# First stage of a hybrid decoder segment on a transposed copy of x, norm factors applied behind the products, and TensorE's order in the attention written by hand

## The chip, the cores and the metric

One core of a Trainium2 chip runs the whole program, a two-layer decoder segment over 1024 tokens of width 1024. The metric is the device time of one execution in microseconds, the median of three runs. TensorE (PE) multiplies, VectorE (DVE), ScalarE (ACT) and GpSimd (POOL) work element by element, and SyncE (SP) issues nearly all DMAs.

## The reference

Layer 0 is sliding-window attention (16 query heads, 2 key heads of 64, window 128, a learned sink per head, partial rotary), layer 1 a gated linear recurrence. Both sit between two RMS norms:

```python
for layer in range(DEPTH):
    h = rmsnorm(x, pre_norm_w[layer])
    y = attention_mixer(h, ...) if layer % 2 == 0 else hgrn2_mixer(h, ...)
    x = x + rmsnorm(y, post_norm_w[layer])

def rmsnorm(x, w):   # float32
    return x * rsqrt(mean(x * x, -1, keepdims=True) + 1e-6) * w

def attention_mixer(h, positions, w_in, b_in, sinks, w_out, b_out):
    q, k, v, z = split(h @ w_in + b_in)          # 1024, 128, 128, 1024 columns
    q, k = partial_rope(q), partial_rope(k)      # first 16 of 64 dims
    o = sliding_window_gqa(q, k, v, sinks)       # 128-query blocks, softmax with sink
    return (o * silu(z)) @ w_out + b_out
```

The factor `rsqrt(mean(x*x))` of a norm is one number per token. A projection is linear in it, so it can be multiplied in before the product or behind it, ahead of the bias.

## The kernel before, in words

All products are float32 made of three float32r matmuls: each operand is held as a high part and a low part (`act[k, half]` as `acth`/`actl`, weights as `whi`/`wlo`), and `product` (line 189) issues high x high, low x high and high x low for one block `k` of 128 rows of the 1024 that are summed over. The tokens are cut into two halves of 512. A unit is one PSUM tile of 128 features x 512 tokens: `proj_feat` runs eight products, 24 matmuls, into it. Weights come in slots of 128 x 512, by DMA into one of four `wraw` buffers; POOL (slots under 20) or ACT makes the high part, DVE subtracts for the low part, into one of ten buffers. A slot is split as soon as a buffer comes free (`advance`, `used`).

The order of instructions on an engine is set by a scheduler in the recording layer, by a simulated timeline and priorities (`hp()` and `tc.high_priority` move instructions ahead). `InOrder` pins an engine's instructions to the order in which they are written; before, this is used on DVE alone, in the head (line 87 is its line in the profile).

The head, before: 128 tokens at a time, the rows of x are loaded (`x_load`), ACT squares and sums them (line 978 for the first half, 225 for the second), POOL takes the power -1/2 (line 217), DVE multiplies the rows (`norm_rows`), TensorE transposes them (line 237: four 128 x 128 transposes for one block `k` of a half, 32 for a half), and ACT and DVE split the transposed block into `acth` (line 179) and `actl` (line 87 or 180), times the norm weight. The units of the head are the values `v_unit(0)`, the four query units `q_unit(0, ct, 0)` of the first key head and the keys `k_unit(0)`. A branch on a flag (`values_load`), computed from the recurrence's bounds in `cst`, stands ahead of both layers: each engine reads it before it goes on.

The attention, before: for each key head `g` and block `b` of 128 queries, two steps (`par`), 32 in all. A step is: scores (eight matmuls, lines 530 and 531), copy and mask on ACT and DVE, maximum, four exponentials on ACT (line 545), division on DVE (line 548), four transposes (line 551), split into `pT` on ACT and DVE, four or five masks on POOL (up to line 570), and the heads (four matmuls, lines 573 to 577), whose result ACT and DVE (lines 578, 579) add up. Between the steps the list `fill` supplies 30 units: keys, values and queries of the second half, all queries of the second key head, and 16 gate units `z_unit`; the numbers in `at` say how many are written behind each block. Four gate units are left behind the attention. `g_split` then makes `act` out of the gated heads, and `out0_first` starts the output projection.

## Time and profile before

| | |
|---|---|
| median of 3 runs | 907.21 us (907.04 to 907.98) |
| profiled execution | 907.38 us, its span 905.7 us |
| granted TensorE clock | 0.997 |
| busy: PE, DVE, ACT, POOL | 883.6, 556.7, 378.2, 330.6 us |
| instructions of PE | 5342 matmuls and transposes |
| moved by DMA | 78.63 MB |

The span runs from the first instruction to the last. A row of the windows gives the busy time of each engine in a stretch and the number of instructions; a row of the timeline begins with the start and the time taken in microseconds, and ends with the idle time before it and what ended it. A busy TensorE need not be at its peak, since matmuls overlap.

### The profile page before, as it was taken

The numbers are of one execution on the slowest core, as the hardware profiler recorded it, in microseconds if no ns is written. First come the engines' busy times: TensorE is split into PE (matmuls) and PEld (weight loads), VectorE is DVE, ScalarE is ACT, GpSimd is POOL, SyncE is SP. The second block draws the span as 40 slices with busy tenths as digits, with TensorE's granted clock in tenths as the row PEclk, the third lists the DMA queues.
The fourth block names the chain that finished last, engine by engine and source line by source line (L and its number), as shares of the span: only waits on it lengthen the run. The fifth ranks groups of instructions, "written<-read, shape, count | busy, mean of one in ns | idle before, by whom it ended". The sixth has DMA issues, their size and how long they took to land.

```text
span 905.7 us, 14367 instructions
## 1 busy us (share of the span) xinstructions
PE 883.6 (98%) x5342; PEld 738.6 (82%) x5342; DVE 556.7 (61%) x919; ACT 378.2 (42%) x982; POOL 330.6 (37%) x498
## 2 busy tenths in 40 slices
PE   5999999999999999999999999999999999999996
PEld 4888888888878888878888888888888788888885
DVE  6879888777788336762278774336877824252333
ACT  6526667666666232543322332423334224251211
POOL 5504466667776003420053522115425433220011
PEclk9999999999999999999999999999999999999998
DMA  8546364522212234531211010210111003031053
GB/s 284 159 146 184 105 184 128 154 56 76 85 37 81 81 93 138 172 122 42 87 50 34 25 47 1 69 58 28 35 47 47 1 1 93 1 110 78 24 185 121
DMA packets 53608, 78.63 MB, mean 87 GB/s; under 512 B 4824, under 2 KB 25048, under 8 KB 53528
## 3 DMA queue, kind: packets, MB, share of 16 engines
q1 hardware_dynamic: 53248, 77.48, 27.6%
q8 instruction: 44, 0.72, 0.3%
q14 instruction: 36, 0.29, 0.1%
q10 hardware_dynamic: 280, 0.13, 0.1%
HBM read 58.89 MB, written 16.88 MB: 84 GB/s over the span
## 4 chain that ended last, share of the span: by engine, by line
PE 76%; DVE 8%; POOL 6%; issue 5%; ACT 2%; DMA 2%; SPq 0%; POOLq 0%; ACTq 0%; DVEq 0%
PE psmm L189 63%; POOL rstd L217 2%; PE psk L853 1%; PE pso L866 1%; PE pss L530 1%; PE pss L531 1%; PE pso L868 1%; PE pst L551 1%; POOL ms L215 1%; ACT sm L545 1%; DVE actl L180 1%; PE pst L847 1%; PE pst L880 1%; DMA o<-in_x 1%; PE psd L804 1%
## 5 line engine op out<-in xcount | busy, mean ns | idle before, releaser
L189 PE MATMUL psmm<-acth,whi 128*128 128x512 f32 x528 | 208.8, 396 | 0.6 <-DVE ql L378 0.3
L189 PE MATMUL psmm<-acth,wlo 128*128 128x512 f32 x528 | 207.8, 394 | 0.2 <-POOL wlo L155 0.2
L189 PE MATMUL psmm<-actl,whi 128*128 128x512 f32 x528 | 207.7, 393 | 0.0
L189 PE MATMUL psmm<-whi,acth 128*128 128x512 f32 (+1 forms) x520 | 202.7, 391 | 0.5 <-DVE y L632 0.5
L189 PE MATMUL psmm<-wlo,acth 128*128 128x512 f32 (+1 forms) x520 | 200.7, 387 | 0.0
L189 PE MATMUL psmm<-whi,actl 128*128 128x512 f32 (+1 forms) x520 | 200.6, 388 | 0.0
L155 DVE TENSOR_TENSOR wlo<-wraw,whi 128x512 fp32r<-128x512 f32 x126 | 94.8, 765 | 93.4 <-ACT whi L154 86.6
L189 PEld LDWEIGHTS psmm<-acth,whi 128*128 128x128 f32 x528 | 99.3, 188 | 20.9 <-DVE qf L706 0.8
L189 PEld LDWEIGHTS psmm<-acth,wlo 128*128 128x128 f32 x528 | 99.2, 188 | 19.9 <-POOL wlo L155 0.6
L189 PEld LDWEIGHTS psmm<-whi,acth 128*128 128x128 f32 x520 | 97.7, 188 | 20.4 <-DVE y L632 0.8
L189 PEld LDWEIGHTS psmm<-actl,whi 128*128 128x128 f32 x528 | 99.2, 188 | 18.2
L189 PEld LDWEIGHTS psmm<-whi,actl 128*128 128x128 f32 x520 | 97.7, 188 | 19.6
L189 PEld LDWEIGHTS psmm<-wlo,acth 128*128 128x128 f32 x520 | 97.8, 188 | 19.2
L154 ACT ACTIVATE whi<-wraw 128x512 fp32r<-128x512 f32 x112 | 70.2, 631 | 87.3 <-PE psmm L189 67.4
L545 ACT ACTIVATE sm<-sm,st 128x129 f32<-128x129 f32 x128 | 50.0, 393 | 56.0 <-DVE st L543 56.0
L714 POOL TENSOR_SCALAR gate<-gate,lbt 128x512 f32<-128x512 f32 x16 | 17.7, 1108 | 119.1 <-ACT gate L712 108.5
L927 DVE TENSOR_TENSOR y<-psmm,wpost 128x512 f32<-128x512 f32 (+1 forms) x17 | 11.2, 660 | 53.7 <-ACT jk L926 50.5
L217 POOL TENSOR_TENSOR rstd<-ms,nhalf 128x1 f32<-128x1 f32 (+1 forms) x48 | 41.7, 870 | 3.8
L562 POOL TENSOR_SCALAR_AFFINE_SELECT mY<-pT 64x256 fp32r<-64x256 f32 x56 | 28.6, 511 | 36.7 <-ACT pT L554 31.0
L926 ACT ACTIVATE jk<-psmm 128x512 f32<-128x512 f32 (+1 forms) x17 | 9.7, 571 | 67.0 <-PE psmm L189 67.0
L179 ACT ACTIVATE acth<-pst,cst 128x512 fp32r<-128x512 f32 x48 | 29.6, 693 | 12.7 <-PE pst L237 12.7
L565 POOL TENSOR_SCALAR_AFFINE_SELECT mY<-pT 64x256 fp32r<-64x256 f32 x64 | 31.8, 496 | 6.9 <-ACT pT L554 1.6
(219 smaller groups left out, 1420.2 us busy)
## 6 DMA issues: line engine op xcount, KB each, us to landing
wraw<-in_w SPq DMA_DIRECT2D x132, 256.0 KB
QS<-qd SPq DMA_DIRECT2D x16, 512.0 KB
xr<-in_x SPq DMA_DIRECT2D x8, 512.0 KB
x1d<-xn SPq DMA_DIRECT2D x8, 512.0 KB
xr<-x1d SPq DMA_DIRECT2D x8, 512.0 KB
out_dram<-xn SPq DMA_DIRECT2D x16, 256.0 KB
xh<-in_x SPq DMA_DIRECT2D x4, 512.0 KB
qd<-qh SPq DMA_DIRECT2D x8, 256.0 KB
```

Source lines behind the costliest of these rows:

```text
L154: nc.scalar.activation(hi, raw, AF.Copy)
L155: W["split_ins"][i] = (nc.gpsimd if on_pool else v).tensor_tensor(lo, raw, hi.bitcast(F32), op=ALU.subtract)
L179: ins = nc.scalar.activation(hi, ps, AF.Copy, scale=scale)
L180: W["actl"][k] = v.scalar_tensor_tensor(lo, ps, scale, hi.bitcast(F32), op0=ALU.mult, op1=ALU.subtract)
L189: W["mm"] = nc.tensor.matmul(ps, a, b, start=(k == 0 and i == 0), stop=(k == NK - 1 and i == 2))
L217: W["rstd"] = keep(nc.gpsimd.tensor_tensor(r, m, nhalf[:, :width], op=ALU.pow))
L545: nc.scalar.activation(sm[:, h, :], sm[:, h, :], AF.Exp, bias=nm[:, h:h + 1], scale=0.125, accum_out=dn[:, h:h + 1])
L562: nc.gpsimd.affine_select(mY[r, :, :64], src[64:, :, :64].bitcast(F32), [[0, 4], [-1, 64]], ALU.is_gt, 0.0, base=0, channel_multiplier=1)
L565: nc.gpsimd.affine_select(mY[r, :, 64:], src[:64, :, 64:].bitcast(F32), [[0, 4], [1, 64]], ALU.is_ge, 0.0, base=0, channel_multiplier=-1)
L714: nc.gpsimd.tensor_scalar(dst, dst, ol, lb, op0=ALU.mult, op1=ALU.add)
L926: nc.scalar.activation(jk[:, c0:c1], ps, AF.Square, scale=D ** -0.5, accum_out=ss)
L927: v.tensor_tensor(y[:, c0:c1], ps, wpost[:, c * 512 + c0:c * 512 + c1], op=ALU.mult)
```

## The change

Head. The host also hands in x transposed (`xt`), and the head loads blocks of it straight into the layout that the products need. `act[k, 0]` is made of unnormalised x times the norm weight. Both first units (values and the first query unit) run side by side, block by block, as `xt` and the first four weight slots land; of slots 0 and 2 the first 128 columns are split first. The rows of x are still loaded, for the sums of squares alone; the factors of 512 tokens are spread over 128 partitions by four transposes of a broadcast column (`spread`), into `rb0` and `rb1`. A unit of the first half is multiplied by `rb0` when it leaves PSUM (`scaled`, one more DVE instruction for each of 18 units). For the second half `xt1` itself is multiplied by `rb1` (`scaled_half`, eight DVE instructions). The rows' buffers are `xt1` and the rotary tables' space, so these are filled only behind the sums. In the head all five engines keep the written order.

Attention. `attn` is cut in three: `scores`, `turned` (transposes, split, masks) and `heads_out`. `later` puts a part on a list with the number of products behind which it is issued: step `i` has its scores behind 25 + 7.3 i products, its transposes 11 and its heads 21 products further on. TensorE's order is pinned as written, through the first four output units. The four gate units that stood behind the attention are now inside it; a gate unit with `p >= 4` now writes the gate alone, and the heads of the second key head are multiplied in behind it, for all eight blocks (before: four). `g_split` of the first half is inside too, and weight splits have no raised priority while the list runs. `tw` has two buffers (one before), `sm` two (three before), `ql` one (two before).

```diff
+        def split_first(i, c0, c1, act=False):
+            hi, lo, raw = whi[i][:, c0:c1], wlo[i][:, c0:c1], wraw[i][:, c0:c1]
...
-                with hp():
-                    on_pool = i in (2, 3)
+                with ExitStack() if W["plan"] else hp():
...
+            W["pos"] += 1
+            while W["plan"] and W["plan"][0][0] <= W["pos"]:
+                W["plan"].pop(0)[1]()
+
+        def later(d, f, block=99):
+            W["plan"].append((W["pos"] + d, f, block))
+            W["plan"].sort(key=lambda e: e[0])
...
+            def scaled(ps, half, t=None):
+                if half:
+                    return ps
+                if t is None:
+                    t = qp.tile([P, 512], F32, tag="th", bufs=2, name="sc")
+                v.tensor_tensor(t, ps, rb0, op=ALU.mult)
+                return t
...
+                def spread(rs, rb):
+                    pt = pp.tile([P, 512], F32, tag="o", name="psr")
+                    for j, r in enumerate(rs):
+                        pe.transpose(pt[:, j * P:(j + 1) * P], r.to_broadcast([P, P]), ident)
+                    ac.activation(rb, pt, AF.Copy)
+
+                def scaled_half(xt, rb, half):
+                    v.on = True
+                    for k in range(NK + 2):
+                        if k < NK:
+                            x = xt[:, k, :]
+                            v.tensor_tensor(x, x, rb, op=ALU.mult)
+                            ac.activation(act[k, half][0], x, AF.Copy, scale=cst[:, C_PRE + k:C_PRE + k + 1])
+                        if k > 1:
+                            act_low(k - 2, half, xt[:, k - 2, :], cst[:, C_PRE + k - 2:C_PRE + k - 1])
+                    v.on = False
...
-                    last = transpose_half(hn0, 0, C_PRE, {2: lambda: advance(4)})
...
+                    for k in range(NK):
...
+                            act_from_psum(k, 0, o0v[:, k, :], cst[:, C_PRE + k:C_PRE + k + 1])
...
+                        for u in range(2):
+                            c = (k % 4) * P
+                            product(first[u], k, weight(2 * u, k // 4, c, c + P), act[k, 0])
+                            used(2 * u + k // 4)
...
+                    rs0 = [row_rstd(sp, rows[0][j], jkb) for j in range(4)]
...
+                    ps2 = proj_feat(q_first(0, 2), 0, "s", {4: first_scaled})
+                    split_next()
+                    rs1 = [row_rstd(sp, rows[1][j], jkb) for j in range(4)]
+                    cs3 = sines()
...
+                    ps3 = proj_feat(q_first(0, 3), 0, "s")
+                    rb1 = sp.tile([P, 512], F32, name="rb1")
+                    spread(rs1, rb1)
...
-                v_unit(0)
-                q_unit(0, 1, 0)
-                transpose_half(hn1, 1, C_PRE)
-                q_unit(0, 2, 0)
...
+                v_unit(0, first[0], sc[0])
+                q_unit(0, 1, 0, first[1], 0, sc[1])
+                q_unit(0, 2, 0, ps2, 2)
+                q_unit(0, 3, 0, ps3, 4)
+                scaled_half(xt1, rb1, 1)
+                q_unit(0, 0, 0, at=6)
...
-                        early = p >= 4 and half == 1
+                        early = p >= 4
...
-                at = [3, 5, 7, 7, 9, 11, 14, 14, 17, 19, 20, 23, 25, 27, 27]
+                fill += zs((4, 0), (4, 1), (5, 0), (5, 1), (6, 0), (7, 0), (6, 1), (7, 1))
+                fill += zs(*[(p, h) for h in range(2) for p in range(4)])
...
+                A0, AP, AT, AV = 25, 7.3, 11, 21
+                W["pos"] = 0
+                for i, (g, b, par) in enumerate((g, b, par) for g, b in order for par in range(2)):
+                    for d, f in ((0, scores), (AT, turned), (AV, heads_out)):
+                        later(A0 + AP * i + d, lambda f=f, g=g, b=b, par=par: at_once(f, g, b, par), 8 * g + b)
...
+        xt_load(o0v, 0, 0)
+        for f in FIRST[:2]:
+            nc.sync.dma_start(wraw[f], I["w"][f])
+        for k in range(1, 4):
+            xt_load(o0v, k, 0)
```

The instructions in the order in which they stand, at three places. First DVE, in the head behind the flag (`o0` holds x, `rt` the rotary angles). Before, the multiplication of the rows comes ahead of the first low parts:

```order
L87 TENSOR_SCALAR o0_136<-o0_136,rstd_168 128x1024
L87 TENSOR_SCALAR rt3_222<-a1r_224 128x64
L87 TENSOR_SCALAR rt3_222<-rt1_220 128x64 x2
L87 TENSOR_SCALAR rt4_223<-rt3_222 128x256
L87 TENSOR_SCALAR o0_136<-o0_136,rstd_176 128x512 x2
L87 TENSOR_TENSOR wlo0_90<-wraw0_100,whi0_80 128x512
L87 SCALAR_TENSOR_TENSOR actl0_0_105<-pst_242,cst_72,acth0_0_104 128x512
L87 SCALAR_TENSOR_TENSOR actl1_0_109<-pst_249,cst_72,acth1_0_108 128x512
```

After, on the same engine at the same place (`o0` holds blocks of transposed x), from the first row behind the flag on:

```order
L87 SCALAR_TENSOR_TENSOR actl0_0_105<-o0_136,cst_72,acth0_0_104 128x512
L87 TENSOR_TENSOR wlo0_90<-wraw0_100,whi0_80 128x128
L87 TENSOR_TENSOR wlo2_92<-wraw2_102,whi2_82 128x128
L87 TENSOR_TENSOR wlo0_90<-wraw0_100,whi0_80 128x384
L87 SCALAR_TENSOR_TENSOR actl1_0_109<-o0_136,cst_72,acth1_0_108 128x512
L87 TENSOR_TENSOR wlo2_92<-wraw2_102,whi2_82 128x384
L87 SCALAR_TENSOR_TENSOR actl2_0_113<-o0_136,cst_72,acth2_0_112 128x512
L87 TENSOR_TENSOR wlo1_91<-wraw1_101,whi1_81 128x512
L87 CAST rt0_200<-pos_74 128x64
L87 TENSOR_SCALAR rt0_200<-rt0_200,cst_72 128x64
L87 SCALAR_TENSOR_TENSOR actl3_0_117<-o0_136,cst_72,acth3_0_116 128x512
```

The row multiplications are gone, the low parts of x and of the first slots alternate, and the rotary steps have moved behind them.

Second DVE again, where the low parts `actl` of the second half are made, for which `k_unit(1)` on TensorE waits. Before, they come straight out of the PSUM tiles `pst` of the transposes, each as soon as its tile is there:

```order
L155 TENSOR_TENSOR kw11_215<-wraw3_103,kw10_214 128x512
L180 SCALAR_TENSOR_TENSOR actl1_1_111<-pst_475,cst_72,acth1_1_110 128x512
L180 SCALAR_TENSOR_TENSOR actl2_1_115<-pst_482,cst_72,acth2_1_114 128x512
L180 SCALAR_TENSOR_TENSOR actl4_1_123<-pst_496,cst_72,acth4_1_122 128x512
L466 TENSOR_TENSOR VX_200<-pst_428,VX_200 128x8x64
L180 SCALAR_TENSOR_TENSOR actl0_1_107<-pst_468,cst_72,acth0_1_106 128x512
L180 SCALAR_TENSOR_TENSOR actl5_1_127<-pst_503,cst_72,acth5_1_126 128x512
L378 SCALAR_TENSOR_TENSOR ql_550<-psmm_524,cst_72,qh_549 128x512
L180 SCALAR_TENSOR_TENSOR actl7_1_135<-pst_517,cst_72,acth7_1_134 128x512
```

After, each block of `xt1` is multiplied by `rb1` first, and the first query unit's own steps (`sc`, `qtB`) stand in between:

```order
L87 TENSOR_TENSOR xt1_206<-xt1_206,rb1_461 128x512 x3
L87 SCALAR_TENSOR_TENSOR actl0_1_107<-xt1_206,cst_72,acth0_1_106 128x512
L87 TENSOR_TENSOR xt1_206<-xt1_206,rb1_461 128x512
L87 SCALAR_TENSOR_TENSOR actl1_1_111<-xt1_206,cst_72,acth1_1_110 128x512
L87 TENSOR_TENSOR xt1_206<-xt1_206,rb1_461 128x512
L397 TENSOR_TENSOR sc_563<-psmm_538,rb0_176 128x512
L87 SCALAR_TENSOR_TENSOR actl2_1_115<-xt1_206,cst_72,acth2_1_114 128x512
L87 TENSOR_TENSOR xt1_206<-xt1_206,rb1_461 128x512
L87 SCALAR_TENSOR_TENSOR actl3_1_119<-xt1_206,cst_72,acth3_1_118 128x512
L87 TENSOR_TENSOR xt1_206<-xt1_206,rb1_461 128x512
L87 SCALAR_TENSOR_TENSOR actl4_1_123<-xt1_206,cst_72,acth4_1_122 128x512
L87 TENSOR_TENSOR xt1_206<-xt1_206,rb1_461 128x512
```

In place of one DVE instruction for a block there are two, and all of them stand behind `rb1`, the spread factors of the second half.

Third TensorE, where the attention's last heads (`pso`) stand. Before, they come among the first output products of the first half (`acth0_0`: block 0, half 0):

```order
L189 MATMUL psmm_3362<-whi6_86,acth0_0_104 128x512
L189 MATMUL psmm_3362<-wlo6_96,acth0_0_104 128x512
L189 MATMUL psmm_3418<-whi6_86,acth0_0_104 128x512
L189 MATMUL psmm_3418<-wlo6_96,acth0_0_104 128x512
L573 MATMUL pso_3179<-pT_3176,VX_200 128x512
L574 MATMUL pso_3179<-pT_3176,VX_200 128x512
L576 MATMUL pso_3179<-mY_3180,tw_2927 128x4x64
L577 MATMUL pso_3179<-mY_3180,VL_201 128x4x64
L189 MATMUL psmm_3362<-whi6_86,actl0_0_105 128x512
L189 MATMUL psmm_3362<-whi7_87,acth1_0_108 128x512
L189 MATMUL psmm_3362<-wlo7_97,acth1_0_108 128x512
L189 MATMUL psmm_3362<-whi7_87,actl1_0_109 128x512
```

After, they come three blocks into the first output unit of the second half (`acth*_1`), whose blocks 4 to 7 are made of those heads:

```order
L217 MATMUL psmm_3477<-whi6_86,acth2_1_114 128x512
L217 MATMUL psmm_3477<-wlo6_96,acth2_1_114 128x512
L217 MATMUL psmm_3477<-whi6_86,actl2_1_115 128x512
L87 MATMUL pso_3439<-pT_3387,VX_182 128x512 x2
L87 MATMUL pso_3439<-mY_3390,tw_3043 128x4x64
L87 MATMUL pso_3439<-mY_3390,VL_183 128x4x64
L217 MATMUL psmm_3477<-whi7_87,acth3_1_118 128x512
L217 MATMUL psmm_3477<-wlo7_97,acth3_1_118 128x512
L217 MATMUL psmm_3477<-whi7_87,actl3_1_119 128x512
L217 MATMUL psmm_3506<-whi4_84,acth0_1_106 128x512
L217 MATMUL psmm_3506<-wlo4_94,acth0_1_106 128x512
L217 MATMUL psmm_3506<-whi4_84,actl0_1_107 128x512
```

The attention has moved back by four units of output products; behind its last heads stand five products, of blocks 0 to 3, until one needs block 4. From there on the instructions of every engine stand in the same order as before, up to the numbers of the weight buffers.

472 lines of the change are left out of this document (282 added, 190 removed).

## The prediction, as it went on record

> **What bounds the kernel now.** I read the page's totals and chain first, then the busy time by stretches, then the timeline of the first 30 us and of two attention steps.
>
> ```profile
> span 905.7 us, 14367 instructions
> PE 883.6 (98%) x5342; PEld 738.6 (82%) x5342; DVE 556.7 (61%) x919; ACT 378.2 (42%) x982; POOL 330.6 (37%) x498
> core 0: us, PE busy (x) PEld busy (x) DVE busy (x) ACT busy (x) POOL busy (x), PEclk, DMA share, GB/s
> 0.00:28.00 28.00, 18.67 (x83) 15.22 (x84) 18.52 (x45) 17.52 (x30) 17.62 (x34) 1.00 0.68 235
> 28.00:65.00 37.00, 36.53 (x180) 30.04 (x178) 29.14 (x49) 14.15 (x23) 9.09 (x16) 1.00 0.61 181
> 65.00:311.00 246.00, 244.79 (x1284) 206.76 (x1283) 198.47 (x367) 154.42 (x462) 144.56 (x251) 1.00 0.37 108
> 253.00:276.00 23.00, 22.00 (x111) 17.63 (x110) 21.29 (x37) 16.63 (x49) 16.90 (x23) 1.00 0.20 54
> 311.00:355.00 44.00, 44.00 (x199) 36.46 (x197) 17.48 (x25) 12.37 (x28) 5.90 (x15) 1.00 0.30 95
> ```
>
> TensorE is the bound. It stands idle for 22.1 us (905.7 less 883.6): 9.3 before 28 us, 0.5 up to 65, 1.2 in the attention (65 to 311), none up to 355, the rest in stages whose instructions keep their order. A change can gain by work taken off TensorE, by an earlier start and by those gaps; another engine counts only where TensorE waits for it. VectorE comes nearest, with 21.3 of 23 us busy around 265 us, just where TensorE loses 1.0.
>
> The unit of account is the product matmul. The first row below is of the chain, the others count the matmuls of line 189 in the same stretches:
>
> ```profile
> 408.60 64.17 PE psmm L189 x283
> 0.00:28.00 28.00, 12.72 (x50) 1.00 0.68 235
> 65.00:311.00 246.00, 193.11 (x771) 1.00 0.37 108
> ```
>
> One takes 64.17 / 283 = 0.227 us. At 28 us, 50 have begun, which is 11.3 us of work.
>
> **The start (to 28 us).**
>
> ```profile
> 5.54 0.17 DVE L966 TENSOR_TENSOR ld<-cst 128x8 f32<-128x8 f32 x1 [5.54 <-DMA cst<-in_cst]
> 6.86 0.14 DVE L972 CAST flag<-ld 1x1 int32<-1x1 f32 x1
> 8.48 0.19 DVE L87 CAST rt<-pos 128x64 f32<-128x64 int32 x1 [1.48 <-DMA pos<-in_pos]
> 9.42 5.38 PE L237 MATMUL pst<-cst,o 128*128 128x128 f32 x24 [3.09 <-DVE o L87]
> 12.26 0.33 POOLq L984
> 13.88 1.08 DVE L87 TENSOR_TENSOR wlo<-wraw,whi 128x512 fp32r<-128x512 f32 x1
> 14.61 1.39 PE L189 MATMUL psmm<-acth,whi 128*128 128x512 f32 x2
> 14.89 2.05 DVE L87 SCALAR_TENSOR_TENSOR actl<-pst,cst,acth 128x512 fp32r<-128x512 f32 x3
> 15.84 0.60 PE L237 MATMUL pst<-cst,o 128*128 128x128 f32 x4
> 16.51 0.39 PE L189 MATMUL psmm<-acth,wlo 128*128 128x512 f32 x1
> ```
>
> The flag is ready at 7.0 (6.86 + 0.14), and reading it holds an engine some 0.3 to 0.5 (the POOLq row). Before, TensorE then waits for POOL's powers and VectorE's row multiplications until 9.42, and its first product starts at 14.61. After, the first product needs the flag, one block of x with its high part made ahead of the flag, and 128 columns of slot 0 split on ScalarE. That gives 7.0 + 0.4 + 0.1, so 7.5; down to 6.6 if the smaller `cst` lands a microsecond before 5.54, up to 8.5 if the first instructions behind the flag wait for a landing as VectorE's did (8.48).
>
> TensorE begins slowly: 24 transposes took 5.38 (0.22 each), the four at 15.84 only 0.60 together; a product matmul 0.39 at 16.51, two at 14.61 took 1.39. From 9.42 to 15.8 it ran at half speed, which cost 3.2 us. It will again, now on products, and I take the same 3.2, with 1.7 and 4.5 as bounds: half of the shortest and all of the longest stretch that these rows allow (3.4 and 4.5, where the waits at 14.6 may count as slow).
>
> The Trainium skill ("TensorE: Matmul & The Clock Gate", Part 1) says that the first 3.4 us or so of activity run at half clock, and its Part 4 that transposes do not count as activity. By that the cold stretch would have begun at 14.61 and lasted to 18.0; the trace disagrees, with full speed at 16.51, 1.9 us after the first product. By the page the new start, all products, would lose 1.7 instead of 3.2 and the sum below would come to 899.3.
>
> So 50 products are begun by 7.5 + 3.2 + 11.3 = 22.0, against 28.0: **-6.0**. Two covers must hold. VectorE must finish eight `actl` (2.05 / 3 = 0.68 each, 5.5), five slot splits (1.08 beside POOL, 5.4) and eight small rotary steps (0.19, 1.5) before the last block: 7.5 + 12.4 = 19.9, plus that block's six products 1.4 is 21.3, 0.7 before TensorE. And the DMA must bring 3.1 MB (eight x blocks, four slots); at the first stretch's 235 GB/s that is 13.2 us, seven before the last block is used. SyncE issues 12 transfers ahead of the flag instead of nine; the four last wait for earlier landings, inside the same seven.
>
> **The second half (28 to 65 us).** The other 32 transposes go, eight come (two spreads):
>
> ```profile
> L237 PE MATMUL pst<-cst,xh 128*128 128x128 f32 x32 | 4.2, 274 | 0.0
> L225 ACT ACTIVATE jkx<-xh 128x1024 f32<-128x1024 f32 x4 | 4.2, 1060 | 0.1
> 26.47 0.69 ACT L442 ACTIVATE vf<-psmm,cst 128x512 f32<-128x512 f32 x1 [0.90 <-PE psmm L189]
> 24.02 1.28 ACT L302 ACT_TABLE_LOAD   x1
> L579 DVE TENSOR_TENSOR o<-pso,ob 64x512 f32<-64x512 f32 x16 | 10.9, 680 | 0.5 <-ACT ob L578 0.2
> ```
>
> 4.2 us less 8/32 of that is **-3.2**. What is late next is `rb1`. TensorE reaches the first spread 15 products into the third unit (21.5 + 3.4 = 24.9, with transposes 25.4), ScalarE copies it by 26.1. In ScalarE's queue then stand, ahead of `rb1`: four square sums (1.06 + 0.19 each, 5.0), five evictions (0.69, 3.5), a table load (1.28), two sines (0.5). So `rb1` is there at 37.0. VectorE then has eight multiplications, eight subtractions and the first query unit's own three steps: 16 x 0.68 + 2.1 = 13.0, the last `actl` at 50.0. TensorE starts `k_unit(1)` behind 144 products: 7.5 + 3.2 + 32.7 + 1.1 + 0.4 = 44.9, and needs block 7 at 49.7. They meet, with VectorE 0.3 late; POOL's splits beside the multiplications can add up to 0.4 (1.08 against 0.68) on some ten of them. I take 1.5 of waiting here, between 0 and 4.3.
>
> The first scores stand 25 products into the next stage, 17 us of cover (44.9 + 1.5 + 17.0 + 0.6 = 64.0), and need the keys: 12 VectorE instructions of the key unit behind 50.0 and seven others in their queue, about 0.7 each, 63.3. I take 0.5 for that, between 0 and 3. Before, this stretch idled 0.5 itself. Stage: -3.2 + 1.5 + 0.5 - 0.5 = **-1.7**. The 2 MB more that are read here (x comes twice) have the sums' 15 us on ScalarE as cover.
>
> **The attention.** One multiplication by `rb0` for 12 units (0.68 from the row above, 8.2 us) and four more gate products less four fewer elsewhere go to VectorE: 198.5 + 8.2 = 207 of 243 us, 85% against 81. Nothing of it is on TensorE, so it costs only where a step is late. What the old steps took, at 171 us and at the crowded end:
>
> ```profile
> 171.07 0.28 PE L531 MATMUL pss<-KL,QS 128*128 128x128 f32 x1
> 177.83 0.68 DVE L548 TENSOR_TENSOR sm<-sm,st 128x512 f32<-128x512 f32 x1
> 181.61 0.60 PE L551 MATMUL pst<-cst,sm 128*128 128x128 f32 x4
> 185.60 0.66 POOL L570 TENSOR_SCALAR_AFFINE_SELECT pT<-pT 128x512 fp32r<-128x512 f32 x1
> 260.34 0.28 PE L531 MATMUL pss<-KL,QS 128*128 128x256 f32 x1
> 270.64 0.69 DVE L548 TENSOR_TENSOR sm<-sm,st 128x512 f32<-128x512 f32 x1
> L573 PE MATMUL pso<-pT,VX x32: 388/397/503, 88.9 to 289.4; 128*128 128x512 f32 x32
> ```
>
> From scores to weights it was 7.2 us (178.51 - 171.35) at 171 and 10.7 (271.33 - 260.62) at 260; from transposes to masks 4.1 (186.26 - 182.21). The new table gives 11 products (7.5) and at least a neighbour's eight scores for the first, 10 products (6.8) and about the same for the second. TensorE's work per step beside products is (244.8 - 771 x 0.227) / 32 = 2.2, so some 1.1 lies in between: 8.6 and 7.9. That is enough at 171 and 2.1 too little at 260. The pace eases, from (289.4 - 88.9) / 31 = 6.5 to 7.3 x 3 x 0.227 + 2.2 = 7.2 us a step. But the last 24 products before the output now hold eight subtractions of `g_split` as well: 3.4 steps of 4.5 us of VectorE, three gate units of 1.6, 5.4 of subtractions, 25.5 us for 24.3 of TensorE. I take 2.0 of waits against the old 1.2: **+0.8**, between -1.2 and +9. The transfers of queries go out a step ahead as before; `ql` with one buffer is refilled a unit (5.4 us or more) later, longer than its store.
>
> **Behind it**, the last heads must pass ScalarE, VectorE twice, ScalarE and VectorE (about 0.6 to 0.7 each, 3.3) before block 4 is used, under five products (3.4): **+0.3**, between 0 and 2. All later stages are carried over.
>
> Sum: -6.0 - 1.7 + 0.8 + 0.3 = -6.6 from the profiled 907.4 (907.38, against a median of 907.21; the 0.2 between them is kept out): **900.8**.
>
> **Rivals.** (a) TensorE's written order makes it stand still with each late step. For it: the 10.7 us at 260 against a room of 8.6, and VectorE's 21.3 of 23. Against it: a slower pace and the middle steps' slack of 1.4. The gain of 6.6 is gone at 0.2 us of waiting more in each of 32 steps; with 0.4 in each the kernel takes 907.4 + 6.2 = 913.6, slower. (b) The head is bound by VectorE and the square sums: `rb1` four or five microseconds later, because the 8.8 MB up to the last row of x come at 235 GB/s (37 us instead of my 31). Then `k_unit(1)` waits 6 instead of 1.5, with a key wait of 3 to follow: 907.8, no change. (c) All goes smoothly: start at 6.6, 1.7 of slow clock, no waits in head or attention: -8.4 - 3.7 - 1.2 = -13.3, 894.1. For it speak the idle VectorE at 46 us and the slower pace.
>
> **How the numbers follow.** 0.2% (1.8 us) is about what a measurement of this kernel can tell from no change. Forecast, 897 to 904.5: 0.55. (c), 891 to 897: 0.15. (b), 904.5 to 909: 0.16, a third of it still faster. (a), above 909: 0.14, a little of it not yet slower. That makes faster 0.76, same 0.11, slower 0.13. From 893 to 907 there lie the forecast, most of (c) and over half of (b), about 0.79.
>
> **What would show it.** The first product of line 87 near 7.5 and 48 of them begun by 21.5; slow ones for the first 6 us. TensorE waiting at `psmm<-acth,kw` of the second half for `actl` by 1 to 2 us near 48. In the attention, waits of TensorE for `sm` (DVE) or `pT` (POOL), 2 us in all, most of them after 240. Output products of the second half starting some 7 us earlier than before. Wrong would be the prediction if the products start later than 9, if the waits in the attention sum to over 6, or if a transfer rather than VectorE ends the waits in the head.

## The result, and the profile after

The changed kernel takes 916.22 us, the median of four runs (915.26 to 917.35), against 907.6 (907.04 to 908.7) of the kernel before beside it: 1.0094 times as long, with an interval of 1.0076 to 1.0111. It is slower by 8.6 us where I had forecast 6.6 us less. The profiled run took 916.49 us, its span 914.8.

First the page's head and the same stretches as before (columns: stretch, its length, busy time and number of instructions of each engine, TensorE's granted clock, DMA share, GB/s):

```profile
span 914.8 us, 14330 instructions
PE 881.2 (96%) x5286; PEld 732.9 (80%) x5286; DVE 573.2 (63%) x940; ACT 382.6 (42%) x984; POOL 337.5 (37%) x498
0.00:28.00 28.00, 20.76 (x82) 15.75 (x83) 21.12 (x50) 14.36 (x24) 13.67 (x29) 1.00 0.93 338
28.00:65.00 37.00, 32.78 (x149) 26.08 (x148) 31.06 (x52) 20.83 (x34) 13.71 (x24) 1.00 0.63 197
65.00:311.00 246.00, 235.40 (x1219) 197.62 (x1218) 204.62 (x371) 150.51 (x452) 147.78 (x241) 0.98 0.37 107
311.00:355.00 44.00, 43.44 (x196) 35.62 (x195) 18.32 (x27) 14.55 (x32) 4.88 (x14) 1.00 0.25 75
```

TensorE has 2.4 us less work than before, but stands idle for 33.6 us instead of 22.1. Two rows tell of it: 4.2 of 37 us idle up to 65 (before 0.5), and 10.6 of 246 in the attention (before 1.2), where the clock is also lower for the first time, 0.98.

Stretches of the clock mix what starts earlier with what runs slower. A better rule is the same piece of work in both traces: I counted the product matmuls (three per block and unit) and noted when the n-th one starts.

| product matmul | before, us | after, us | after - before | gained or lost since the row above |
|---|---|---|---|---|
| first | 14.61 | 7.36 | -7.3 | |
| 144 (`k_unit(1)` begins) | 54.05 | 44.28 | -9.8 | -2.5 |
| 168 (attention begins) | 59.49 | 53.54 | -6.0 | +3.8 |
| 312 | 103.12 | 96.91 | -6.2 | -0.3 |
| 384 | 126.05 | 125.80 | -0.3 | +6.0 |
| 1152 (attention is over) | 354.99 | 364.27 | +9.3 | +9.5 |
| last | 897.02 | 906.16 | +9.1 | -0.1 |

So the head gained what it should, 9.8 us up to the 144th product; 3.8 went at once in one unit, and 15.2 (6.0 + 9.5 - 0.3) in the attention, of which 6.0 fall on 72 product matmuls between 97 and 126 us. The stages behind run as before.

Equal numbers of products are not quite equal work, though: the other matmuls, 16 for each step and a few transposes of the values, fall into these stretches as each kernel orders them, before 82, 49 and 387 of them, after 63, 52 and 403. With these taken at the usual intervals of the trace of before (0.11 to 0.23 us each), the three stretches of the attention lose 2.4, 5.4 and 7.4 us, the same 15.2 in all: the -0.3 up to the 312th hides a loss of 2.4 behind work that was put off.

TensorE's waits after the start, in the attention and its neighbours (what it waited for: us in all, times, the longest):

```profile
PE pst L87 <- DVE sm L704: 10.1, 5, 4.6
PE psmm L87 <- DVE actl L87: 2.0, 1, 2.0
PE psmm L87 <- DVE sc L397: 1.3, 1, 1.3
PE pst L87 <- POOL vmid L591: 0.9, 1, 0.9
PE pst L87 <- ACT acth L780: 0.5, 1, 0.5
```

Five waits of the transposes for `sm`, the divided weights, make 10.1 us. They are few and long, the longest two at these places:

```profile
101.91 0.63 PE L87 MATMUL pst<-cst,sm 128*128 128x128 f32 x4 [3.45 <-DVE sm L704]
272.52 1.08 PE L87 MATMUL pst<-cst,sm 128*128 128x128 f32 x4 [4.61 <-DVE sm L704]
103.00:107.00 4.00, 4.00 (x13) 3.18 (x13) 3.91 (x8) 2.42 (x11) 3.02 (x5) 0.57 0.28 93
272.00:278.00 6.00, 5.48 (x17) 4.55 (x18) 5.07 (x10) 1.23 (x2) 3.90 (x7) 0.55 0.36 89
```

Behind each long wait TensorE runs near half clock for some 3 to 5 us (0.57 and 0.55 in the two stretches), though nothing more is late. Summed over the attention, the time from one matmul's start to the next beyond its usual interval is 13.3 us of idle and 3.4 of slow clock, against 2.2 and 0.3 before; that is 14.2 of the 15.2.

Why `sm` is late is read in VectorE's queue. Step 3 (the first is 0) starts its scores at 87.82; its maximum, `st`, is the row at 95.94, its division the one at 101.09:

```profile
87.82 0.28 PE L87 MATMUL pss<-KH,QS 128*128 128x256 f32 x1
90.90 1.40 DVE L565 TENSOR_TENSOR KL<-kft,KH 64x512 fp32r<-64x512 f32 x2
92.33 0.68 DVE L747 TENSOR_TENSOR o<-pso,ob 64x512 f32<-64x512 f32 x1
92.94 0.77 DVE L694 COPY_PREDICATED sm<-msk,pss 128x256 f32<-128x256 uint8 x2
93.61 0.67 DVE L179 TENSOR_TENSOR wlo<-wraw,whi 128x512 fp32r<-128x512 f32 x1
94.31 1.60 DVE L423 TENSOR_TENSOR qtB<-qf,sinT 64x512 f32<-64x512 f32 x2
95.94 0.69 DVE L698 TENSOR_REDUCE st<-sm 128x4 f32<-128x516 f32 x1
...
100.10 0.68 DVE L397 TENSOR_TENSOR sc<-psmm,rb 128x512 f32<-128x512 f32 x1
100.70 0.16 DVE L703 RECIPROCAL st<-st 128x4 f32<-128x4 f32 x1
100.78 0.41 DVE L694 COPY_PREDICATED sm<-msk,pss 128x256 f32<-128x256 uint8 x1
101.09 0.68 DVE L704 TENSOR_TENSOR sm<-sm,st 128x512 f32<-128x512 f32 x1
```

From the scores' start to the divided weights it is 13.95 us (101.77 - 87.82). In between VectorE does the keys' low parts, another step's heads, a weight split, rotary work and two copies of a neighbour step (99.77 and 100.78): all in a queue that is worked off in order. TensorE's written order leaves room for 33 product matmuls with a neighbour's eight scores, 10.65 us here without the wait.

### The profile page after: what moved, and what is told of

The parts are those of the page before. It is cut to its first block, busy times and chain, and to the rows that moved or that the text cites. A ratio compares the mean times of both kernels' runs of the same rounds, so it can differ in the third digit from the quotient of the medians.

```text
span 914.8 us, 14330 instructions
## 1 busy us (share of the span) xinstructions
PE 881.2 (96%) x5286; PEld 732.9 (80%) x5286; DVE 573.2 (63%) x940; ACT 382.6 (42%) x984; POOL 337.5 (37%) x498
## 4 chain that ended last, share of the span: by engine, by line
PE 71%; DVE 10%; POOL 5%; issue 4%; ACT 2%; DMA 1%; POOLq 0%; SPq 0%; DVEq 0%; ACTq 0%
PE psmm L217 47%; PE psmm L87 12%; PE pss L87 2%; PE pso L87 2%; POOL rstd L255 2%; PE psk L1032 1%; PE pso L1045 1%; PE pst L87 1%; PE pso L1047 1%; ACT sm L701 1%; POOL ms L253 1%; DMA qd<-ql 1%; PE pst L1026 1%; PE pst L1059 1%; DVE wlo L179 1%
## 5 line engine op out<-in xcount | busy, mean ns | idle before, releaser
L217 PE MATMUL psmm<-whi,acth 128*128 128x512 f32 (+1 forms) x488 | 190.4, 391 | 1.0 <-DVE y L811 1.0
L217 PE MATMUL psmm<-wlo,acth 128*128 128x512 f32 (+1 forms) x488 | 188.7, 387 | 0.0
L217 PE MATMUL psmm<-whi,actl 128*128 128x512 f32 (+1 forms) x488 | 188.7, 388 | 0.0
L179 DVE TENSOR_TENSOR wlo<-wraw,whi 128x512 fp32r<-128x512 f32 x120 | 87.9, 744 | 92.4 <-ACT whi L178 85.9
L87 PE MATMUL psmm<-acth,whi 128*128 128x512 f32 x264 | 108.6, 411 | 3.0 <-ACT whi L87 1.7
L217 PEld LDWEIGHTS psmm<-whi,acth 128*128 128x128 f32 x488 | 91.7, 188 | 20.3 <-DVE y L811 1.8
L217 PEld LDWEIGHTS psmm<-whi,actl 128*128 128x128 f32 x488 | 91.7, 188 | 18.2
L217 PEld LDWEIGHTS psmm<-wlo,acth 128*128 128x128 f32 x488 | 91.8, 188 | 17.9
L217 PE MATMUL psmm<-acth,whi 128*128 128x512 f32 x264 | 104.4, 396 | 0.2 <-DVE qf L885 0.2
L217 PEld LDWEIGHTS psmm<-acth,whi 128*128 128x128 f32 x264 | 49.6, 188 | 11.1 <-DVE qf L885 0.9
L217 PEld LDWEIGHTS psmm<-acth,wlo 128*128 128x128 f32 x264 | 49.6, 188 | 10.4
```

Of the source, the lines that this page charges most:

```text
L87: return (lambda *a, **k: self.tc.keep_in_program_order(f(*a, **k))) if self.on else f
L179: W["split_ins"][i] = v.tensor_tensor(lo, raw, hi.bitcast(F32), op=ALU.subtract)
L217: W["mm"] = pe.matmul(ps, a, b, start=(k == 0 and i == 0), stop=(k == NK - 1 and i == 2))
```

## The experiments

Every time below stands beside runs of the kernel before on the same chip (907.6 to 908.07 us). Three columns give the time from the 168th product matmul to the 312th, from there to the 384th, and to the 1152nd. Before, these are 43.6, 22.9 and 228.9; the last column is the excess over their sum, 295.5. The steps' own matmuls are in these times; the second table takes them out for six kernels.

| kernel | us | ratio (interval) | 168-312 | 312-384 | 384-1152 | excess |
|---|---|---|---|---|---|---|
| changed kernel | 916.22 | 1.0094 (1.0076-1.0111) | 43.4 | 28.9 | 238.5 | 15.2 |
| e1 head only | 913.10 | 1.0064 (1.0047-1.0080) | 42.1 | 35.0 | 230.9 | 12.5 |
| e2 room | 914.82 | 1.0082 (1.0065-1.0099) | 42.8 | 27.4 | 236.9 | 11.6 |
| e3 split behind | 918.63 | 1.0121 (1.0104-1.0138) | 43.4 | 30.1 | 239.4 | 17.4 |
| e4 kept busy | 915.71 | 1.0091 (1.0075-1.0108) | 43.5 | 26.6 | 239.6 | 14.2 |
| e5 attention only | 920.73 | 1.0142 (1.0125-1.0159) | 40.6 | 27.1 | 239.3 | 11.5 |
| e6 no factors | 918.92 | 1.0131 (1.0114-1.0148) | 40.6 | 27.1 | 239.7 | 11.9 |
| e7 POOL multiplies | 919.26 | 1.0131 (1.0114-1.0148) | 43.7 | 29.1 | 238.3 | 15.5 |
| e8 rotary apart | 923.26 | 1.0180 (1.0158-1.0201) | 43.2 | 31.5 | 241.5 | 20.7 |
| e9 e8's order on e1 | 917.50 | 1.0099 (1.0077-1.0120) | 45.0 | 28.9 | 237.2 | 15.6 |
| e10 pace by load | 921.67 | 1.0148 (1.0131-1.0165) | 41.9 | 31.4 | 241.5 | 19.3 |
| e11 e2 + e8 + e10 | 915.89 | 1.0093 (1.0074-1.0112) | 41.4 | 25.8 | 241.6 | 13.4 |
| e12 e1 without factors | 917.78 | 1.0115 (1.0098-1.0132) | 41.5 | 38.9 | 229.7 | 14.7 |
| e13 without factors | 917.18 | 1.0103 (1.0087-1.0120) | 42.9 | 29.7 | 239.3 | 16.4 |
| e14 order not pinned | 919.36 | 1.0123 (1.0106-1.0140) | 42.0 | 22.5 | 249.2 | 18.2 |
| e15 gates behind | 923.66 | 1.0168 (1.0146-1.0190) | 45.3 | 29.5 | 240.3 | 19.6 |
| e16 old places, new head | 922.13 | 1.0161 (1.0144-1.0178) | 45.4 | 25.8 | 244.8 | 20.5 |
| e17 old places, old head | 918.91 | 1.0114 (1.0095-1.0133) | 45.1 | 25.2 | 234.4 | 9.2 |
| e18 head only, order mended | 908.78 | 1.0013 (1.0004-1.0022) | 42.1 | 30.6 | 230.6 | 7.8 |

| kernel | the steps' own matmuls in the three stretches | lost beyond them, us |
|---|---|---|
| before | 82, 49, 387 | |
| changed kernel | 63, 52, 403 | 2.4, 5.4, 7.4 |
| e1 | 58, 81, 379 | 1.7, 8.0, 2.9 |
| e2 | 63, 48, 407 | 1.8, 4.4, 5.4 |
| e14 | 48, 47, 423 | 3.0, -0.4, 15.6 |
| e17 | 83, 52, 383 | 1.4, 1.9, 5.9 |
| e18 | 58, 65, 395 | 1.7, 5.6, 0.4 |

**Which part (e1, e5).** e1 keeps the new head and takes the attention of before (`attn` uncut, the list `at`, TensorE's order left to the scheduler, `tw` one and `sm` three buffers); e5 is the reverse.

> The new head with the attention of before: its 32 steps whole, TensorE's order left to the scheduler, the old list of units, four gate units behind; the multiplication by the factors of the first half stays (it belongs to the head). Theory: the loss is made in the attention by its written order. Then the matmuls of the first scores start some 6 us earlier than before, as in the changed kernel, no wait of TensorE in the attention is over 1.5 us, and the time is 900 to 903. Rival: the loss is VectorE's load, 12 multiplications by the factors, whatever orders TensorE. Then the waits come here too and the time is 907 or more.

> The head of before (rows normalised, then transposed by TensorE; no factors to apply) with the changed attention: three parts at fixed products, TensorE as written, all 16 gate units and the first half's splitting inside. It tells what the attention's change is worth by itself, since the new head with the old attention took 913.1. Theory, VectorE is the bound from 46 to 112 us and again from 255 to 305: the first stretch has 24 VectorE instructions of 0.65 us less than the changed kernel, so no wait over 2 us there; the second keeps its load and its waits of about 5 us with the slow clock behind: 909 to 912. Rival: the factors alone make the loss, also at the end (8 gate units are multiplied by them there): 904 to 907.

Both parts alone are slower than before, by 5.3 us and 12.9, and together by 8.6: the parts do not add up. (Of e5's 12.9, 2.2 arise ahead of the attention, where this build has one `ql` buffer beside the old head; TensorE's waits there are 1.0 us for `ql` and 0.9 for `lm`.) In e1 the attention loses 12.5 us too, and nearly all of it, 12.1, between the 312th and the 384th product. Of these, 4.1 are the matmuls of two steps more than before; the other 8.0 are for the most part the first wait below, at 110.6 us, the longest of the second row, at 104.9, and the half clock behind them:

```profile
PE pss L683 <- DVE sm L691: 3.4, 1, 3.4
PE pso L726 <- POOL pT L723: 2.6, 4, 1.2
```

So TensorE's pinned order cannot be the whole cause. Behind the 384th product e1 loses only 2.9 us beyond the steps' own matmuls, against 7.4 in the changed kernel: that part belongs to the new attention.

**Room, the late split, and the clock (e2, e3, e4).**

```diff
-                A0, AP, AT, AV = 25, 7.3, 11, 21
+                A0, AP, AT, AV = 25, 7.3, 14, 23          # e2
```
```diff
+                        with ExitStack() if half or p < 4 else tc.issue_after(W["exp"].ins):   # e3, in g_split
                             nc.scalar.activation(hi, o, AF.Copy)
                             v.tensor_tensor(lo, o, hi.bitcast(F32), op=ALU.subtract)
```
```diff
+                    for _ in range({3: 15, 26: 20}.get(2 * order.index((g, b)) + par, 0)):     # e4, in turned
+                        pe.matmul(pt.rearrange("p h q -> p (h q)"), act[0, 1][0][:, :P], act[0, 1][0], start=True, stop=True)
                     for h in range(4):
                         pe.transpose(pt[:, h, :], sm[:, h, :P], ident)
```

> One line: a step's transposes 14 products behind its scores instead of 11, its heads 23 instead of 21, so 12.7 us of room from the first score to the transposes instead of 10.6. Theory: the waits at 98 and 268 us (3.45 and 4.61 us) are late weights against a fixed room; with 2.1 us more both fall to 1.4 and 2.5, the clock stays at full speed behind them (3.9 us lost there now), and the time is 908 (916.2 - 4.2 - 3.9). Rival: whatever room there is, VectorE's queue fills it with work that stands ahead of the weights, and the waits stay above 3: 914 to 917.

> The four last blocks that the first half's splitting takes (acth and actl out of the gated heads of the second key head) are issued behind the exponentials of a later step instead of ahead of those of the step that is waited for at 268 us; TensorE's rows stay the same. Theory: ScalarE's 2.2 us and VectorE's 3.4 us of them made that step's weights late; the wait of 4.61 us falls under 1.5, the slow clock behind it (2.2 us lost) goes, and the time is 911 (916.2 - 3.3 - 2.2). Rival: the step is late through the general load of VectorE, some other work takes the place, the wait stays over 3 and the time at 915 to 917.

> Ahead of the transposes of the two steps that TensorE waits for longest, 15 and 20 more product matmuls of 0.227 us are written, into the PSUM tile that the transposes overwrite, with operands that are long there: TensorE works through the wait instead of standing still. Theory: the half speed behind both waits comes from standing still for 3.4 us and more. Then the clock stays at 1.00 at 103 to 107 and at 272 to 278, and 1.5 + 2.2 us are gained though more work is done: 912.5. Rival: the slow clock has another source (the total load, a fixed time), stays where it is, and the extra matmuls cost nothing or up to a microsecond: 916 to 917.

e2 gives each step nine product matmuls more between scores and transposes. In its profile the waits for `sm` fall from 10.1 to 4.4 us and 3.6 of the 15.2 come back; but that is the quickest of its four executions (913.24), and the times, 914.82 against 916.22, have intervals that overlap. The forecast of 908 was a miss. e3 takes four blocks of `g_split` out of step 26's way. The wait of 4.61 falls to 2.19 and another grows behind it:

```profile
PE pst L87 <- DVE sm L704: 4.9, 3, 3.4
PE pst L87 <- ACT whi L178: 4.0, 1, 4.0
PE pst L87 <- ACT sm L690: 2.2, 1, 2.2
```

The kernel is slower for it, 918.63. e4 fills the two longest waits with 35 matmuls that nobody needs. The same two stretches as above:

```profile
103.00:107.00 4.00, 4.00 (x24) 3.49 (x23) 3.94 (x8) 3.81 (x13) 1.54 (x3) 1.00 0.23 73
272.00:278.00 6.00, 6.00 (x32) 5.11 (x31) 4.13 (x9) 4.15 (x14) 3.25 (x5) 1.00 0.14 46
PE pso L87 <- POOL pT L730: 1.8, 1, 1.8
PE pss L87 <- DMA QS<-qd: 1.4, 1, 1.4
```

The clock is full, 1.00 for 0.57 and 0.55: the slow stretch is a consequence of the wait, not of the work that follows. But the time is no other (915.71). The excess of 14.2 holds 7.9 us of the added matmuls, which stand where waits of 8.1 were, so that only the slow clock could come back; and two new waits stand against it, 1.8 us for masks at 290 us, with half clock behind it, and 1.4 for queries at 68.6, ahead of the first added matmul and so not its doing.

**VectorE's added multiplications (e6, e7, e12, e13).** e6 leaves out the multiplications by `rb0` and `rb1`, 24 of 26 (the two first units keep theirs), and so the norm of most units; e13 those of the units in the attention, e12 is e13 on e1's kernel; e7 gives half of the eight by `rb1` to POOL.

```diff
             def scaled(ps, half, t=None):
-                if half:
+                if half or W["att"]:                      # e13, e12; in e6 always
                     return ps
```
```diff
-                            v.tensor_tensor(x, x, rb, op=ALU.mult)
+                            (nc.gpsimd if k % 2 else v).tensor_tensor(x, x, rb, op=ALU.mult)    # e7
```

> The changed kernel without the multiplications by the factors (16 units of the first half, eight blocks of the second): VectorE has 24 instructions of 0.65 us less; the factors are still made. Left out is thereby the normalisation of most units. Theory: VectorE's load is what gives back the start's lead: the waits for actl (2.0 us), sc (1.3), vmid and the step at 98 us (3.45 and the slow clock behind) go, the one at 268 shrinks: 899 to 904. Rival: the written order with its 10.6 us of room is what TensorE waits for: the head's 3.5 us go, the rest stays: 911 to 914.

> Four of the eight multiplications of the second half's x by its factors go from VectorE to GpSimd, which is busy 13.7 of 37 us there. Theory of VectorE's load: 2.6 us less in its queue; the two waits of the key unit (2.0 and 1.3 us) lose 1.5 to 2.5 us together, and the step at 98 us loses as much of its 3.45 and stays under the length that brings the slow clock: 911 to 914. Rival: the waits there come from the factors' own chain (rows, square sums, spread), which ends at 36.9 whatever multiplies: no change, 915.5 to 917.

> The new head with the old attention (913.1), and the 12 multiplications by the factors that lie in the attention left out (four query units, eight gate units; those of the head stay, so TensorE comes as early). That kernel lost 12.5 us against before between the first product of the second half's values and the end of the attention. Theory, VectorE's load: with 7.4 us of its work gone, two thirds or more of the 12.5 go: 903 to 906. Rival, the lead: VectorE cannot follow a TensorE that comes 6 to 8 us earlier, whatever the 12 cost: the loss stays over 8 and the time at 909 or more.

> The same 12 multiplications left out of the changed kernel, the head as it is. It lost 15.2 us in that stretch; with no factors at all it was 11.9, in the kernel with the new attention alone 11.5. Theory: the new attention loses some 11.5 by itself and the 12 multiplications 3.5 more, so 912 to 914. Rival: the earlier figure was disturbed by that kernel's own wait in the head, and the load is most of the loss: 907 or less.

Taking 12 multiplications off VectorE in the attention gains nothing (e13 917.18 against 916.22; e12 917.78 against e1's 913.10), nor does POOL's help in the head (919.26). e6, which has none in the attention and two in the head, has an excess of 11.9 in the attention instead of 15.2. That is the excess of e5, whose old head needs no factors either, and the two share the waits for `sm` to 0.1 us, the longest of 5.2 at the same place:

```profile
PE pst L87 <- DVE sm L578: 10.4, 5, 5.2
PE pst L87 <- DVE sm L698: 10.4, 5, 5.2
```

The first row is e5's, the second e6's. So 10.4 us of waits come without any multiplication in the attention. Up to the 384th product e6 loses 4.6 us less than the changed kernel and behind it 1.2 more; whether the missing factors give the 4.6 or its later start of the attention (58.6 instead of 53.5: its head got a wait of its own, 3.2 us for `rstd`, and slow clock), these runs don't tell. The twelve multiplications in the attention are not the cause. VectorE's busy share agrees: from the 312th to the 384th product, before, changed kernel, e13:

```profile
103.12:126.05 22.93, 22.92 (x123) 19.30 (x122) 21.15 (x40) 14.85 (x45) 9.63 (x15) 1.00 0.54 157
96.91:125.80 28.89, 25.15 (x125) 20.67 (x124) 25.68 (x49) 18.50 (x56) 17.30 (x25) 0.94 0.41 119
95.73:125.46 29.73, 25.29 (x125) 20.66 (x123) 24.92 (x47) 18.65 (x57) 16.76 (x26) 0.94 0.43 126
```

Before, VectorE is 92% busy and TensorE never waits; after, 89 and 84% busy, and TensorE loses six. The share of VectorE tells nothing here; what differs is that 47 to 49 VectorE instructions and 25 or 26 POOL instructions fall on the same 72 products that had 40 and 15. Whether that is a cause (other work was moved here) or a result (a longer stretch lets more of it run) the counts can't tell. The next group tried the former.

**Moving work out of the stretch (e8 to e11).** e8 changes the order of the eight query units of the second head so that rotary work is spread; e9 does the same on e1; e10 spaces the steps by what stands beside them; e11 puts e2, e8 and e10 together, with `g_split(1)` issued behind the attention.

```diff
-for ct in (0, 1, 2, 3) for h in range(2)]
+for ct, h in ((1, 0), (0, 0), (1, 1), (2, 0), (2, 1), (0, 1), (3, 0), (3, 1))]     # e8
```
```diff
+                PACES = ((8, 8.5), (16, 6.3), (7, 8.2))     # e10: so many steps, products a step
```

> One list: the two rotary query units of the second key head (five or six VectorE steps each instead of one or two) no longer stand next to each other behind the one of the first key head, where the changed kernel has three in a row with the low parts of the keys; they come second and sixth of eight. Theory, VectorE's local load: the waits with and without the factors were the same to 0.1 us, so the step at 98 us is late because VectorE has more work there than the steps' even pace leaves. Then that wait (3.45 us and 1.7 of slow clock) falls to under 1 in all, the one at 268 stays, and the time is 911 to 913. Rival: the room of 10.6 us is too small for the first steps whatever stands there; the wait moves by a step or two and the time stays at 915 to 917.

> The same list in the kernel with the new head and the old attention (913.1), whose largest waits (3.4 and 2.6 us, and 3 of slow clock) lie between 103 and 118 us, at the same three units. Theory, VectorE's local load: 6 to 8 of its loss of 12.5 us in the attention go, and the time is 905 to 907. Rival: the lead of the head is lost because VectorE has too much work in all up to there (52 of 65 us busy against 48 before): the waits spread over the steps behind and the time stays above 910.

> The 32 steps no longer 7.3 products apart all along, but 8.5 for the first eight, 6.3 for the next 16, 8.2 for the last: the same number in all. VectorE was busy 96% from 65 to 115 us, 80% from 150 to 240 and 97% from 260 to 300. Theory, VectorE's local load against an even pace: both waits lose half or more, 3 to 6 us with the slow clock: 910 to 913. Rival: the waits come from single long pieces in the queues (splitting the gated heads, three rotary units), not from the mean load: 915 to 917.

> Together: rotary units apart, the pace by load, 14 products instead of 11 from scores to transposes (heads at 23), and the second half's splitting kept behind the attention instead of in its last steps. Theory, local load and room: nearly all waits in the attention go (11 to 13 of the 15 us that it loses against before), the head's 3.5 stay: 902 to 905, faster than before. Rival, what is taken from one place comes back at the next: no less than 908.

These were misses. e8 and e10 are slower than their rivals had it, too: they lengthen the stretch that they were to relieve (31.5 and 31.4 us for 28.9), and the kernel by 7.0 and 5.5 us. e9 shortens it in e1 (28.9 for 35.0) and loses more around it. e11 is no better than the changed kernel, and its stretch of 25.8 is close to the 27.4 that e2's larger room gives alone. The theory of a local overload of VectorE found no support in them.

**The order on each engine (e14 to e17).** e14 leaves TensorE's order in the attention to the scheduler (`pe.on = True` taken out). e15 puts the gate units and `g_split` behind the attention, as before. e16 and e17 put each step's scores, transposes and heads at the very product numbers that they have before, on the new head and on the old.

```diff
-                    for d, f in ((0, scores), (AT, turned), (AV, heads_out)):
-                        later(A0 + AP * i + d, lambda f=f, ...
+                    for d, f in zip(TABLE[i], (scores, turned, heads_out)):     # e16, e17
+                        later(d, lambda f=f, ...
```

> The changed kernel with TensorE's order in the attention left to the scheduler; the three parts, the units and their places are written as before. Theory: TensorE's pinned order turns each late step into a wait; free, TensorE takes products ahead as in the old kernel, and half or more of the 15.2 us lost there go: 904 to 909. Rival: VectorE is late on its own account, and the scheduler, which does not know of it, sets much the same order: 913 to 917.

> The changed kernel with the four gate units of the first half's second key head and the first half's splitting behind the other units again, as in the old attention (their gate multiplied in on VectorE at once); the steps are 6.3 products apart, so that they end by the same unit as before. TensorE's order stays pinned. Theory: the loss at the end (waits and slow clock from 255 to 305 us, 9.0 us there) comes from that work moved into the last steps: 6 or more go, 908 to 911. Rival: at 6.3 products a step VectorE is the bound all along, the waits spread over the middle: 916 or more.

> The new head, and the attention's machinery of the changed kernel (three parts, TensorE pinned), but each step's scores, transposes and heads stand behind the very product behind which they stand in the kernel before (from the first transposes on; the first five scores a little later, since the keys come after), the gate units and the first half's splitting behind again, three weight buffers and one tw. From scores to transposes there are then 13 to 19 products in most steps instead of 11. Theory, room and places: with before's places for TensorE the attention loses no more than 4 us instead of 15.2, the lead of the head stays, and the time is 900 to 906. Rival: TensorE's places are not it; ScalarE and VectorE execute in an order that is set ahead too, and that order (new head, parts issued at once) makes the steps late: 911 or more.

> The same with the head of before: TensorE's instructions in the attention now stand as before to within a product, only the way in which they are written (three parts, pinned) and so the order on ScalarE and VectorE differ. Theory, room and places: nothing is left that could wait, 906 to 910, as before. Rival, the order on ScalarE and VectorE: waits of 5 us and more in the steps and 913 or more.

From the 312th to the 384th product e14 has no wait at all and is as quick as before (22.5 us), but only 38 VectorE and 15 POOL instructions run there, as before. It takes 20.3 us more later, 4.6 of them the steps' own matmuls that it does there and before did ahead, the others lost, among them six waits for POOL's masks (5.1 us) and one for `acth` (2.8). e15 and e16 came out as their rivals had it, at 923.66 and 922.13: both wait 4.3 us for `acth` where the first half's splitting now ends the attention (at 307 and 306 us), e15 4.5 more for `actl` at 52. e17 is the sharpest of them: head as before, and on TensorE the attention's parts at the old products; yet its kernel takes 11 us longer, and in its profile, the slowest of four executions that spread from 915.83 to 920.27, the attention takes 9.2 more, with 3.4 ahead of it behind a wait for `ql`, which has one buffer:

```profile
PE pso L87 <- POOL pT L603: 3.8, 5, 1.3
PE psmm L190 <- DVE ql L386: 2.3, 1, 2.3
PE psmm L87 <- ACT acth L655: 2.1, 1, 2.1
PE pss L87 <- DVE sm L569: 1.6, 2, 1.4
```

TensorE's places are thus not enough. What its waits name are results of POOL, ScalarE and VectorE, whose order the scheduler sets anew for each build. That points at their order. But e17 differs from before in more than order: `ql` has one buffer, the gate units' `th` shares the buffers of `qh`, and weight splits have no raised priority. None of these was varied alone, and I did not pin the three engines to the order of before, so whether it is their order, and which rows, stays open.

**The best of them (e18).** In e1 the scheduler had put the scores of steps 6 and 7 both behind the 336th product matmul. e18 mends that: `ql` with two buffers, as before (dynamic DMA scratch cut from 1024 to 256 for the space), and the query units in the order (0,0), (1,0), (1,1), (0,1), then (2,0) and on.

> The new head with the old attention (913.1, of whose loss 12.1 us lie between the 312th and the 384th product matmul, where TensorE's rows have the scores of two steps behind the same product and 24 matmuls of room) with two edits: two ql buffers as before, and one of the two rotary query units of the second key head two units later. TensorE's rows then have at least 11 product matmuls between two steps' scores and 37 to 67 of room behind the fifth step, as before. Theory, order: the local loss of that stretch shrinks from 12 to 2 to 4 us, the rest of the attention stays as before, the lead of the head (8 us at the 312th) is kept for the most part: 901 to 905. Rival, as with before's places for TensorE: VectorE and ScalarE, set ahead in an order of their own, are late anyway and the loss moves on: 910 or more.

Product matmuls between a step's scores and its transposes, counted in the programs, for steps 4 to 9:

```
before           43 53 55 44 42 43
changed kernel   33 33 33 33 33 33
e1               29 37 24 48 48 24
e18              29 37 45 50 44 43
```

With steps 6 and 9 given back their room, the time falls from 913.1 to 908.78 (11 runs, 907.89 to 909.79), 1.0013 of before with an interval of 1.0004 to 1.0022. The wait of 3.4 us in e1 was of step 7's scores, right behind those of step 6, until VectorE had copied earlier scores (`sm`) out of PSUM; with the two steps apart it is gone. The second `ql` buffer came in the same run, so its share is not known; the waits for `ql` are 1.2 us in e1 and 0.7 in e18. e18 leads by 8.1 us at the 312th product (94.97 for 103.12), 3.2 of it by step matmuls put off; it gives back 7.7 up to the 384th, of which 2.0 are a step's matmuls done there and 5.6 are lost, and 1.6 behind. No version here beats the kernel before.

## Why the prediction was wrong, step by step

**The start: right, with one term too large.** First product at 7.36 (7.5 forecast), 48 begun by 21.09 (21.5), slow clock up to 11.1. The slow clock cost about 2.0 us and not 3.2: the first eight products took 4.0 us for 1.8 at full speed, 0.16 of it a wait. Small delays behind it, 0.6 in all, and the first product 0.14 early leave the sum close to the forecast. By the 144th product the gain is 9.8 us, where the start and the spared transposes made 9.2. The DMA moved 338 GB/s instead of 235, and no wait of TensorE in the head was ended by a transfer.

```profile
7.36 0.80 PE L87 MATMUL psmm<-acth,whi 128*128 128x512 f32 x1 [1.70 <-ACT whi L87]
11.12 0.42 PE L87 MATMUL psmm<-actl,whi 128*128 128x512 f32 x1
36.31 0.60 ACT L87 ACTIVATE rb<-psr 128x512 f32<-128x512 f32 x1 [1.14 <-PE psr L87]
50.09 0.50 PE L87 MATMUL psmm<-actl,kw 128*128 128x512 f32 x1 [2.02 <-DVE actl L87]
53.54 0.50 PE L87 MATMUL psmm<-acth,whi 128*128 128x512 f32 x1 [1.33 <-DVE sc L397]
```

**`k_unit(1)`: right place and cause, too small.** `rb1` is there at 36.9 (37.0 forecast) and `actl` is what TensorE waits for, but the unit is 3.8 us late instead of 1.5, within the bounds of 0 and 4.3. I had left out that the next unit's PSUM tile is only freed by a `sc` in the same VectorE queue: 1.3 of it.

**The attention: the step that failed.** The term was +0.8, bounds -1.2 to +9; it measured 15.2. Rival (a) had the direction, not the form: six late steps, not 0.4 us in each of 32. Three things made it up.

First, I had read two of the 32 steps of before, both by the time from the end of the scores to the weights. The reading at 171 was near enough: the division at 177.83 belongs to scores that began at 164.59, and their second half was done by 170.90, or by 171.35 if it is the one that I took, so the step took 7.2 to 7.6 us. The middle steps (8 to 23) were in time, as forecast. The steps that I had not read are those ahead of 130 us. Step 6 is an example, with its last scores and its division in the last two rows:

```profile
164.59 0.23 PE L530 MATMUL pss<-KH,QS 128*128 128x128 f32 x1
170.62 0.28 PE L531 MATMUL pss<-KL,QS 128*128 128x128 f32 x1
105.89 0.28 PE L531 MATMUL pss<-KL,QS 128*128 128x256 f32 x1
119.55 0.72 DVE L548 TENSOR_TENSOR sm<-sm,st 128x512 f32<-128x512 f32 x1
```

That is 14.1 us (120.27 - 106.17), and steps 4, 5 and 7 took 11.1 to 11.6. The new room, which I gave as 8.6, measured 9.6 from the end of the scores (10.6 from their start): by these rows the first steps were at risk too. Three of them are late: the waits at 77.78, 101.91 and 125.42 are 4.9 us. At the crowded end I had found the room 2.1 us too small for a step, which was right, and yet had put 2.0 us of waits for the whole attention; there the waits are 5.7 (272.52, 290.13 and 297.74).

Second, the latency of a step was taken as a number. It is what the queues leave: from the start of the scores 5.7 to 9 us in the middle steps of the changed kernel, 13.95 and 15.2 in the two that TensorE waits for longest. The wait at 272.52 comes from other work issued ahead of the step on ScalarE and VectorE:

```profile
264.54 2.19 ACT L780 ACTIVATE acth<-og 128x512 fp32r<-128x512 f32 x4 [1.97 <-DVE og L749]
267.35 0.41 ACT L701 ACTIVATE sm<-sm,st 128x129 f32<-128x129 f32 x1
267.14 3.36 DVE L781 TENSOR_TENSOR actl<-og,acth 128x512 fp32r<-128x512 f32 x4
270.43 1.13 DVE L179 TENSOR_TENSOR wlo<-wraw,whi 128x512 fp32r<-128x512 f32 x1
271.48 0.17 DVE L703 RECIPROCAL st<-st 128x4 f32<-128x4 f32 x1
271.68 0.69 DVE L704 TENSOR_TENSOR sm<-sm,st 128x512 f32<-128x512 f32 x1
```

The exponentials wait behind four `acth`, the reciprocal behind four `actl` and a split. I had counted that work (25.5 us of VectorE for 24.3 of TensorE) as a balance of sums; in order, it comes as a block of 3.36 ahead of the one instruction that TensorE needs. e3 took that block away, and the wait was 2.19 instead of 4.61 with others behind it. The multiplications, which I let "cost only where a step is late", cost nothing that can be measured even so: without them nothing is won (e13).

Third, a wait had no price beyond itself. 3.4 us of the attention's loss are slow clock behind the waits, an effect that I had used for the start alone; e4 shows it, since there the same two stretches run at full clock.

**Behind it: right.** From the 1152nd product to the last it takes 542.0 us before and 541.9 after. The +0.3 for the last heads stands ahead of that; TensorE waits for no part of block 4 there.

**What would show it.** The products began before 9 and VectorE, for the first product ScalarE, and no transfer ended the waits in the head, as forecast; the attention's waits summed to over 6, which I had named as the sign of a wrong prediction.

**What stays open.** That TensorE waits for late weights against a fixed room in the changed kernel is shown by its waits and by e2's profile, where three products more of room cut them from 10.1 to 4.4 us; that more room makes the kernel faster is not (914.82 against 916.22). That the place of the steps' scores is part of the loss is shown for e1 alone, by e18 and the wait that is gone there. That the order on ScalarE, VectorE and POOL is the rest is what e14 and e17 leave, and is argued, not shown. A rival that no run tests alone are the buffers: `ql` has one in every build but before and e18, and `sm` has two in the changed kernel. Why the 72 products behind the 312th lose up to 10.7 us (e12) beyond the steps' own matmuls, in all builds but e14 and the filled e4, is not settled.
